# Storing the tokens' 1/rms straight from VectorE's result, number by number

## The chip, the cores and the metric

The kernel runs on one core of a Trainium2 chip. Its engines are TensorE (matmul; PE in the profile), VectorE (DVE), ScalarE (ACT), GpSimd (POOL) and SyncE (SP), each with its own list of instructions that it works off in order, and 16 DMA engines that move data. SP, ScalarE and GpSimd issue DMAs. On-chip data lies in SBUF (128 partitions); TensorE writes into PSUM, which has eight banks of 128 x 512 numbers here. The metric is the device time of one execution in microseconds (us); lower is better.

## What is computed

One layer of a decoder trunk, for 1,024 tokens of 1,024 channels, all in float32. Cut to its core:

```
h = rmsnorm(x, norm_g) * (1 + scale) + shift        # scale, shift, gate from silu(c) @ mod_w
cv, cg, cs, lx, ls = split(h @ w_in)
v = layernorm(depthwise_conv31(cv * sigmoid(cg)))
y_conv = (silu(v) @ pw2 + pw2_b) * silu(cs)
y_lru = scan(gates(depthwise_conv4(lx))) * silu(ls)
x = x + (1 + gate) * (concat(y_conv, y_lru) @ w_out)
return rmsnorm(x, final_g)
```

`rmsnorm` divides each token by the root of its mean square over the channels: x * rsqrt(mean(x * x) + 1e-6). The change is in how those 1,024 numbers, one for each token, get to where they are needed.

## The kernel before

**Layout.** Channels lie on the partitions and tokens along the free dimension: `x` is eight tiles of 128 channels x 1,024 tokens. Each float32 matmul is made of three: weights and activations are split into a high and a low part (`whi`, `wlo`; `uh`, `ul`), and high x high, high x low and low x high are added up in PSUM. One output tile (128 x 1,024, two banks of 512 tokens) takes 2 x 8 x 3 = 48 matmuls of 128 x 512.

**The start.** To keep TensorE busy from the beginning, the first seven tiles of h @ w_in are made without the tokens' 1/rms: `FIRST` (four tiles, `first0` to `first3`, L805) and `NEXT` (`ps4` to `ps6`, L506) multiply x * g * (1 + scale), and 1/rms is multiplied in afterwards, on VectorE, as the product is read out of PSUM (`first_u<-first,rbc`, `next<-ps,rbc`, both L374). The shift's share is a bias, summed in `fsum` on VectorE and added up over channels by TensorE (`psbias`, L1011). From tile 7 on, the activations themselves are normalised: VectorE multiplies x by `rbc` (L366), ScalarE and VectorE split them into `uh` and `ul` again. The second half of `first3` finds no free bank at first; it is computed afterwards as `late`, once ScalarE has copied the first half of `first3` out.

**From the squares to `rbc`.** The steps that the change touches:

- VectorE sums the squares of the eight tiles (`sq`); TensorE sums them over the channels (`token_stats`, L949) into `psb`, 128 tokens x 8 blocks: token b * 128 + p stands on partition p in column b.
- ScalarE takes the root (`st`, L355), VectorE its reciprocal in place (L957).
- TensorE turns `st` round with a matmul by the identity (`turn`, L960): 8 rows of 128 tokens, in the same bank `psb`.
- ScalarE copies the 8 rows out of PSUM into the first rows of `rbc` (L347), and its queue stores them to DRAM (`rrowd`, L964), 8 rows of 512 bytes.
- SP's queue loads the 1,024 numbers back, broadcast to all 128 partitions: `rbc`, 128 x 1,024 (L965, through the helper at L395).

**What sets the order.** The whole program is first written down as operations with an engine, a cost, a priority and what they read and write (`S.op` and the helpers ACT, TT, STT, DMA). The planner (`Plan.order`) then runs them through a list scheduler on its estimated costs and emits every engine's list in the order that comes out. PSUM banks and buffers are given out in that order too, as they come free. A change of a cost or of an operation can therefore move other instructions anywhere behind it. The numbers of the plan around the change: the operation of the store has a cost of 0.3 on ScalarE and a `lag` of 0.1, after which its data counts as written.

The core of it:

```
spread = S.op("PE", 0.2, turn, RSP, [("st", 0)], wk, columns=4 * P)
spread_out = ACT(RSP, row, lambda: psb()[:KT, P:2 * P], "copy", P, r=wk, w=[(rbc, 0)])
S.op("ACT", 0.3, lambda: act.dma_start(flat, row()), RSP, [(rbc, 0)], [("rrowd", 0)], lag=0.1)
DMA(RSP, rbc, lambda: flat.rearrange("b p -> (b p)").partition_broadcast(P), FULL_BYTES,
    r=[("rrowd", 0)], w=[rbc])
```

Of the kernel before, what the change touches and what calls it, by code (L numbers as in the profile page):

```python
# [9 lines left out]
F32 = mybir.dt.float32  # L10
# [4 lines left out]
P = 128  # L15
D = 1024
T = 1024
KT = D // P
# [44 lines left out]
BYPOOL = {512: (0, 1), 768: ()}  # L63
PWE = ((None, None), (None, None), (None, None), ((2, 6), (1, 0)))
REV = -1
OUT_ORDER = (0, 1, 2, 3, 6, 5, 4, 7)
SUMS = (2, 6, 1, 4, 3, 0, 7, 5)
QRES = 0
# [25 lines left out]
SQP, RSP, BIP, HHP, HCH, EVP = -84, -110, -50, -56, 0.1, -80  # L94
# [210 lines left out]
def hymba_layer(ctx: ExitStack, tc: tile.TileContext, xT, xa, vecs, mod_w, mod_s0, w_first, w_pairs, w_in,  # L305
# [3 lines left out]
    act, dve, pool, pe, sp = nc.scalar, nc.vector, nc.gpsimd, nc.tensor, nc.sync  # L309
# [7 lines left out]
    dram = ctx.enter_context(tc.tile_pool(name="dram", bufs=1, space=bass.MemoryType.DRAM))  # L317
# [11 lines left out]
    S = Plan(pools)  # L329
# [11 lines left out]
    def ACT(prio, out, in_, func, n=T, bias=None, scale=None, accum=None, r=(), w=(),  # L341
            reserve=0, after=()):
        kw = {}

        def emit():
            if func == "copy":
                act.copy(out(), in_())  # L347
                return
            if bias is not None:
                kw["bias"] = bias  # L350
            if scale is not None:
                kw["scale"] = scale
            if accum is not None:
                kw["accum_out"] = accum
            act.activation(out=out(), in_=in_(), func=func, **kw)  # L355
        ptr = sum(x is not None and not isinstance(x, float) for x in (bias, scale))
        return S.op("ACT", a_cost(n, ptr) + (0.1 if accum is not None else 0), emit, prio, r, w,
                    table=SETS.get(func), reserve=reserve, after=after)
# [77 lines left out]
    ident = const.tile([P, P], F32, tag="ident", name="ident")  # L436
# [304 lines left out]
    psb = bank("token_stats")  # L741
# [26 lines left out]
    after = []  # L768
    for z, (a, e) in enumerate(CPARTS):
        if e == T:  # L770
            after = [S.op("PE", 0.22 * (e - a) / P, scale_mm, -130,
                          [("cs", 0), *halves(modt[KT], a, e)], [ps_g], after=after, columns=4 * (e - a))]
        after = [S.op("PE", 0.22 * (e - a) / P, lambda z=z: spread_c(z), -130, [("cs", 0)],
                      [ps_c[z]], after=after, columns=4 * (e - a))]
# [43 lines left out]
    for i, ld in enumerate(LOADS):  # L818
        p = due[ld] = i - 100.0
# [5 lines left out]
        elif ld[0] in "wW":  # L825
# [6 lines left out]
                w=keys(rw))  # L832
            for j in range(k, k + nk):
# [3 lines left out]
                for a, e in ((0, FW // 2), (FW // 2, FW)) if j == 0 else ((0, FW),):  # L837
                    ACT(p, fw_part(hi, j, a, e), fw_part(rw, j, a, e), "copy", e - a, r=[(rw, jj)],
                        w=fw_keys(hi, j, a, e))
                if j:  # L840
                    SUB(p, "DVE", fw_part(lo, j), fw_part(rw, j), fw_part(hi, j), FW,
                        r=[(rw, jj), *fw_keys(hi, j)], w=fw_keys(lo, j))
# [35 lines left out]
    for k in range(KT):  # L878
        p = due[f"s{k}"]
# [9 lines left out]
        p = max(p, due[f"x{k}"] if k else p, due[f"w{k}"])  # L889
# [4 lines left out]
        for a, e in START if k < UK else ((0, T),):  # L894
            n = e - a
            hk = halves(x_, a, e)
            if k == 0 == a:
                o = TS(p, part(uh, a, e), part(x_, a, e), g, None, ALU.mult, n=n,
                       r=hk + [("gs", k)], w=halves(uh, a, e))
# [34 lines left out]
    for k in range(KT):  # L934
        p = SQP + k
# [20 lines left out]
               scale=1.0 / D, r=wk, w=[("st", 0)])  # L956
    S.op("DVE", 0.2, lambda: dve.reciprocal(st, st), RSP, [("st", 0)], [("st", 0)])  # L957

    def turn():
        pe.matmul(psb()[:KT, P:2 * P], st, ident, start=True, stop=True)  # L960
    spread = S.op("PE", 0.2, turn, RSP, [("st", 0)], wk, columns=4 * P)
    row, flat = lambda: rbc()[:KT, :P], dram.tile([KT, P], F32, tag="rrow", name="rrowd")
    spread_out = ACT(RSP, row, lambda: psb()[:KT, P:2 * P], "copy", P, r=wk, w=[(rbc, 0)])
    S.op("ACT", 0.3, lambda: act.dma_start(flat, row()), RSP, [(rbc, 0)], [("rrowd", 0)], lag=0.1)  # L964
    DMA(RSP, rbc, lambda: flat.rearrange("b p -> (b p)").partition_broadcast(P), FULL_BYTES,  # L965
        r=[("rrowd", 0)], w=[rbc])

# [359 lines left out]
    for i, (s, ps) in enumerate(zip(FIRST, psf)):  # L1327
        j, p, bi = s[1] % KT, EVP + i, bias[:, i:i + 1]
        t = big_buf(f"first_u{i}", parts=4)
        for a, e in START:  # L1330
            tk, pk, n = halves(t, a, e), halves(ps, a, e), e - a
            if (a, e) in cuts[i]:
                alone = len(cuts[i]) == 1
                if alone:
                    ACT(RSP, part(t, a, e), part(ps, a, e), "copy", n, r=pk, w=tk)
                TT(p - 4 * alone, "DVE", part(t, a, e), part(t if alone else ps, a, e),
                   part(rbc, a, e), ALU.mult, n, r=(tk if alone else pk) + halves(rbc, a, e),
                   w=tk).slack = RBC_LAG
            else:
                late = bank("late")  # L1340
                for k in range(KT):
                    fw_mm(RSP + 60 + 0.1 * k, late, i, uhs[k], uls[k], k, ((a, e),),
                          after=[spread], off=a)
                TT(p, "DVE", part(t, a, e), part(late, 0, n), part(rbc, a, e), ALU.mult, n,
                   r=[late] + halves(rbc, a, e), w=tk)
            if s[1] < CG:
                if a == 0:
                    v[j] = big_buf(f"v{j}")
                STT(p + 3, apart(v[j], a, e), by_two(t, a, e), bi, by_two(sig[j], a, e), ALU.add,
                    ALU.mult, n, r=tk + halves(sig[j], a, e) + [("bias", 0)], w=[v[j]])  # L1350
        if s[1] >= CG:
            ACT(p + 3, t, t, AF.Sigmoid, bias=bi, r=[t, ("bias", 0)], w=[t])
            sig[j] = t
# [303 lines left out]
```

## Time and profile before

| | |
|---|---|
| time, median of 3 runs | 727.56 us (727.23 to 727.83) |
| the profiled execution, its own time | 727.49 us |
| its span, first to last instruction | 725.5 us |
| TensorE's mean granted clock | 0.998 |
| VectorE, ScalarE, GpSimd busy | 87%, 65%, 13% of the span |
| moved by DMA | 112.10 MB |

The profile is one execution. It has the busy time of each engine, the chain of work that ended last (followed back from the last instruction, at each step to what released it), groups of instructions by line, waits, and a timeline. In a timeline's row stand the start, the length, the engine, the line of the kernel, the operation, what it writes and reads (`out<-in`, buffer numbers left out), and in brackets the idle time of the engine ahead of it with what ended it. PEld is the load of weights into TensorE, which overlaps the matmuls. ACTq and SPq are the issues of DMAs. The length of a matmul includes its way through the array, so the pace of a row of matmuls is read from their starts.

### The profile page before, as it was taken

To read this page: it belongs to the slowest core of one execution; us is meant where nothing else is said; L and a number is where in the kernel's file an instruction comes from. 1 tells how busy PE (TensorE), PEld (TensorE's weight loads), DVE (VectorE), ACT (ScalarE), POOL (GpSimd) and SP (SyncE) were. 2 spreads that over 40 slices of the span, in tenths; PEclk is the share of its full clock that TensorE was granted. 3 is DMA by queue.
4 is the path that set the end of the run, shared out by engine and by line. 5 is a ranking of instruction groups with operands and counts; after the bars stand their busy time and mean duration, and the time that the engine had idled before them with its cause. 6 is when DMAs were issued, how large, how long until landed. Compare 5 with 4: busy or idle time off the path is not lost.

```text
span 725.5 us, 8895 instructions
## 1 busy us (share of the span) xinstructions
PE 717.6 (99%) x3250; PEld 597.2 (82%) x3250; DVE 634.4 (87%) x898; ACT 469.9 (65%) x653; POOL 97.5 (13%) x105
## 2 busy tenths in 40 slices
PE   9999999999999999999999999999999999999996
PEld 7888888888888888888888888888888888888886
DVE  6978999999989987787899995998999766997757
ACT  7663766777877878947758885835764334645443
POOL 0042013121232332232021100000000000000001
PEclk9999999999999999999999999999999999999999
DMA  8971026588699799698784545243332530434216
GB/s 334 407 265 63 1 94 136 137 190 190 144 254 239 152 222 221 144 204 169 175 172 101 111 88 161 88 174 134 127 117 77 212 116 2 159 111 137 60 57 232
DMA packets 36634, 112.10 MB, mean 155 GB/s; under 512 B 4072, under 2 KB 10992, under 8 KB 36592
## 3 DMA queue, kind: packets, MB, share of 16 engines
q1 hardware_dynamic: 23760, 76.89, 29.8%
q0 software_dynamic: 12528, 34.26, 26.2%
q8 instruction: 25, 0.41, 0.2%
q10 hardware_dynamic: 304, 0.40, 0.2%
q14 instruction: 17, 0.14, 0.1%
HBM read 64.69 MB, written 12.59 MB: 107 GB/s over the span
## 4 chain that ended last, share of the span: by engine, by line
PE 99%; DVE 0%; ACT 0%; DVEq 0%; issue 0%
PE ps L506 66%; PE first L805 5%; PE pbpw L617 3%; PE pupw L617 3%; PE papw L617 3%; PE gate L1246 3%; PE out L687 2%; PE puout L617 2%; PE paout L617 2%; PE pcpw L617 1%; PE pb0out L617 1%; PE pcout L617 1%; PE late L805 1%; PE out6b L687 1%; PE c_row L757 0%; PE pb1out L617 0%
## 5 line engine op out<-in xcount | busy, mean ns | idle before, releaser
L506 PE MATMUL ps<-uh,whi 128*128 128x512 f32 x576 | 224.2, 389 | 0.0
L506 PE MATMUL ps<-ul,whi 128*128 128x512 f32 x576 | 224.2, 389 | 0.0
L506 PE MATMUL ps<-uh,wlo 128*128 128x512 f32 x576 | 224.2, 389 | 0.0
L506 PEld LDWEIGHTS ps<-uh,wlo 128*128 128x128 f32 x576 | 108.1, 188 | 22.5
L506 PEld LDWEIGHTS ps<-ul,whi 128*128 128x128 f32 x576 | 108.1, 188 | 22.4
L506 PEld LDWEIGHTS ps<-uh,whi 128*128 128x128 f32 x576 | 108.1, 188 | 22.3
L347 ACT CAST whi<-raw 128x1024 fp32r<-128x1024 f32 x46 | 47.9, 1046 | 35.7 <-PE ps L506 30.4
L355 ACT ACT_TABLE_LOAD x47 | 60.3, 1283 | 5.5 <-PE ps L506 3.4
L374 DVE TENSOR_TENSOR wlo<-raw,whi 128x1024 fp32r<-128x1024 f32 x39 | 47.5, 1218 | 17.2 <-ACT whi L347 17.1
L379 POOL DMA_DIRECT2D es<-cq x45 | 39.6, 894 | 152.5 <-ACT cq L355 84.9
L366 DVE SCALAR_TENSOR_TENSOR cacc<-v,V,cacc 128x511 f32<-128x511 f32 (+14 forms) x75 | 55.5, 740 | 0.5
L366 DVE SCALAR_TENSOR_TENSOR caccs<-v,V,caccs 128x511 f32<-128x511 f32 (+6 forms) x70 | 52.1, 744 | 1.4
L366 DVE SCALAR_TENSOR_TENSOR caccs<-c,wsum,caccs 128x511 f32<-128x511 f32 (+6 forms) x70 | 51.9, 741 | 0.6
L379 POOL DMA_DIRECT2D oo<-co x42 | 39.9, 949 | 90.9 <-ACT co L355 61.3
L506 PE MATMUL ps<-yh,wlo 128*128 128x512 f32 x128 | 49.8, 389 | 0.0
L506 PE MATMUL ps<-yh,whi 128*128 128x512 f32 x128 | 49.8, 389 | 0.0
L506 PE MATMUL ps<-yl,whi 128*128 128x512 f32 x128 | 49.8, 389 | 0.0
L374 POOL TENSOR_TENSOR fg<-fg,bc 128x512 f32<-128x512 f32 x2 | 2.5, 1280 | 281.5 <-ACT bc L347 281.5
L366 DVE SCALAR_TENSOR_TENSOR xs<-ps,V,xs 128x512 f32<-128x512 f32 (+3 forms) x48 | 35.7, 743 | 0.2
L355 ACT ACTIVATE cq<-v,V 128x511 f32<-128x511 f32 (+14 forms) x45 | 31.7, 710 | 0.0
L366 DVE SCALAR_TENSOR_TENSOR modw<-modw,sc 128x1024 f32<-128x1024 f32 x23 | 30.1, 1313 | 0.4 <-DMA modw<-in_mod_w_dram 0.4
L355 ACT ACTIVATE cq<-c,wsum 128x512 f32<-128x512 f32 x42 | 29.9, 714 | 0.0
(385 smaller groups left out, 1444.7 us busy)
## 6 DMA issues: line engine op xcount, KB each, us to landing
raw<-in_w_in_dram SPq DMA_DIRECT2D x36, 512.0 KB, 5.2
modw<-in_mod_w_dram SPq DMA_DIRECT2D x23, 512.0 KB, 9.1
raw<-in_w_out_dram SPq DMA_DIRECT2D x10, 512.0 KB, 3.6
scsd<-scs SPq DMA_DIRECT2D x8, 512.0 KB, 3.8
acc<-in_xT_dram SPq DMA_DIRECT2D x8, 512.0 KB, 4.6
accd<-acc SPq DMA_DIRECT2D x8, 512.0 KB, 2.6
rawpw<-in_pw_dram SPq DMA_DIRECT2D x8, 512.0 KB, 3.3
scsr<-scsd SPq DMA_DIRECT2D x8, 512.0 KB, 6.1
```

Of the source, the lines that this page charges most:

```text
L347: act.copy(out(), in_())
L355: act.activation(out=out(), in_=in_(), func=func, **kw)
L366: dve.scalar_tensor_tensor(out=out(), in0=in0(), scalar=scalar, in1=in1(), op0=op0, op1=op1, accum_out=accum)
L374: lambda: e.tensor_tensor(out=out(), in0=a(), in1=b(), op=op), prio, r, w,
L379: return S.op("POOL", ISSUE, lambda: pool.dma_start(out(), a(), accum_op=ALU.add), prio, r, w, lag=RATE * n / T, after=after)
L506: pe.matmul(part(ps, a - off, b - off)(), k3(lhs)()[:, k, :], rhs[k]()[:, a:b], start=(k == 0 and lhs is wh and rhs is xh and (a - off) % ...
L617: pe.matmul(part(ps, 0, c1 - c0)(), half(*lhs)()[:, j * P:j * P + P], half(*rhs)()[:, c0:c1], start=start and j == 0 and z == 0, stop=j == ...
L687: pe.matmul(part(ps, a - off, e - off)(), k3(lhs)()[:, k, :], rhs()[:, i * H + a % H:i * H + a % H + e - a], start=k == KORD[0] and lhs is ...
L805: pe.matmul(part(ps, a - off, b - off)(), fw_part(lhs, k, i * P, i * P + P)(), rhs()[:, a:b], start=k == 0 and lhs is wh and rhs is xh, st ...
L1246: pe.matmul(ps(), lhs()[:, j, :], rhs()[:, c0:c1], start=st == 0, stop=st == 2)
```

## The change

The turn by TensorE and the copy out of PSUM go. The store takes `st` itself, 128 partitions x 8 numbers, and writes each number to its place in the 8 x 128 table in DRAM, so that neighbouring numbers of a partition land 512 bytes apart. The load that broadcasts the table is as before. In the plan the store now has a `lag` of 0.6, and the two operations that were ordered behind the turn or the copy (`late`, and the weights of `NEXT`) are ordered behind the root and the store.

```diff
+SCATTER = 0.6
...
-    def turn():
-        pe.matmul(psb()[:KT, P:2 * P], st, ident, start=True, stop=True)
-    spread = S.op("PE", 0.2, turn, RSP, [("st", 0)], wk, columns=4 * P)
-    row, flat = lambda: rbc()[:KT, :P], dram.tile([KT, P], F32, tag="rrow", name="rrowd")
-    spread_out = ACT(RSP, row, lambda: psb()[:KT, P:2 * P], "copy", P, r=wk, w=[(rbc, 0)])
-    S.op("ACT", 0.3, lambda: act.dma_start(flat, row()), RSP, [(rbc, 0)], [("rrowd", 0)], lag=0.1)
+    flat = dram.tile([KT, P], F32, tag="rrow", name="rrowd")
+    spread_out = S.op("ACT", 0.3, lambda: act.dma_start(flat.rearrange("b p -> p b"), st), RSP,
+                      [("st", 0)], [("rrowd", 0)], lag=SCATTER)
     DMA(RSP, rbc, lambda: flat.rearrange("b p -> (b p)").partition_broadcast(P), FULL_BYTES,
         r=[("rrowd", 0)], w=[rbc])
...
-                          after=[spread], off=a)
+                          after=[root], off=a)
```

The planner moves instructions with it. ScalarE's list from the root on, before (`whi` is the high part of a weight tile, `raw` the tile as loaded, `ghi` the same for the gates; the last number of a name is only a running number, and lines from the store on stand a few further up after the change):

```order
L355 ACTIVATE st_99<-token_stats_120,eps_t_88 128x8
L347 CAST whi4_520<-raw4_442 128x1024
L347 CAST whi7_529<-raw7_476 128x1024
L347 COPY rbc_539<-token_stats_120 8x128
L347 CAST whi8_541<-raw8_482 128x1024
L964 DMA rrowd_100<-rbc_539 8x128
L347 CAST ghi1_551<-graw1_493 128x256
```

and with the change:

```order
L356 ACTIVATE st_99<-token_stats_120,eps_t_88 128x8
L348 CAST whi4_520<-raw4_442 128x1024
L961 DMA rrowd_100<-st_99 128x8x1
L348 CAST whi7_534<-raw7_476 128x1024
L348 CAST whi8_541<-raw8_482 128x1024
L348 CAST ghi1_550<-graw1_493 128x256
```

The store stands behind one cast instead of three, and the copy is gone. VectorE's list where `rbc` is first read, before (`modw3` is the last dot product ahead of it; `next4` the first product of `NEXT`):

```order
L366 SCALAR_TENSOR_TENSOR modw3_406,macc_93<-modw3_406,sc_152 128x1024
L374 TENSOR_TENSOR first_u3_491<-late_543,rbc_539 128x512
L374 TENSOR_TENSOR first_u0_602<-first0_0_171,rbc_539 128x512
L374 TENSOR_TENSOR first_u0_602<-first0_1_202,rbc_539 128x512
L374 TENSOR_TENSOR first_u1_611<-first1_0_173,rbc_539 128x512
```

and with the change:

```order
L367 SCALAR_TENSOR_TENSOR modw3_406,macc_93<-modw3_406,sc_152 128x1024
L375 TENSOR_TENSOR first_u0_596<-first0_0_171,rbc_539 128x512
L375 TENSOR_TENSOR first_u0_596<-first0_1_202,rbc_539 128x512
L375 TENSOR_TENSOR first_u1_602<-first1_0_173,rbc_539 128x512
L375 TENSOR_TENSOR first_u1_602<-first1_1_204,rbc_539 128x512
L375 TENSOR_TENSOR first_u2_613<-first2_0_179,rbc_539 128x512
L375 TENSOR_TENSOR first_u2_613<-first2_1_207,rbc_539 128x512
L375 TENSOR_TENSOR first_u3_491<-late_543,rbc_539 128x512
```

The product of `late` moves from the first place to behind the six others. With it the banks change hands: the bank that `ps4_1` (the second half of tile 4) takes was that of `late`, and is now that of `first0_0`. TensorE's list at the sums of the bias, before:

```order
L506 MATMUL ps6_0_759<-uh1_217,wlo6_613 128x512
L1011 MATMUL psbias_771<-ones_84,fsum_514 128x1 x7
L506 MATMUL ps6_0_759<-uh2_261,whi6_575 128x512
L506 MATMUL ps6_0_759<-ul2_273,whi6_575 128x512
L506 MATMUL ps6_0_759<-uh2_261,wlo6_613 128x512
```

and with the change:

```order
L507 MATMUL ps6_0_756<-uh2_261,wlo6_611 128x512
L507 MATMUL ps6_0_756<-uh3_292,whi6_573 128x512
L507 MATMUL ps6_0_756<-ul3_306,whi6_573 128x512
L507 MATMUL ps6_0_756<-uh3_292,wlo6_611 128x512
L1009 MATMUL psbias_777<-ones_84,fsum_514 128x1 x7
L507 MATMUL ps6_0_756<-uh4_337,whi6_573 128x512
```

The sums stand behind four channel tiles of `ps6_0` instead of two, six matmuls later. Further down, VectorE's and ScalarE's lists differ by neighbours that change places, and TensorE's by three matmuls at two places near its tiles 40 and 41; the load of `rbc` keeps its place on SP.

## The prediction

> **What bounds the kernel now.** I read the page's parts 1 and 4 first (busy time, and the chain that ended last), then what TensorE waited for, then the chain around the changed steps.
>
> ```profile
> span 725.5 us, 8895 instructions
> PE 717.6 (99%) x3250; PEld 597.2 (82%) x3250; DVE 634.4 (87%) x898; ACT 469.9 (65%) x653; POOL 97.5 (13%) x105
> ...
> PE 99%; DVE 0%; ACT 0%; DVEq 0%; issue 0%
> ```
>
> TensorE is busy for 717.6 of 725.5 us, and the chain that ended last is TensorE's own list for 99% of it. A busy engine may still be held up inside its list, so the second view is what it waited for, in the whole span:
>
> ```profile
> PE token_stats L752 <- DVE ones L439: 1.1, 1, 1.1
> PE first L805 <- ACT fhi L347: 0.6, 1, 0.6
> ```
>
> Two waits, both in the first microseconds. So whatever VectorE, ScalarE and the DMA queues do in the middle of this kernel is covered, and a saving there alone is worth nothing. Time is won by taking work out of TensorE's list, and lost by making TensorE wait. The chain around the changed steps, in order of time (start, length, what):
>
> ```profile
> 44.33 2.21 PE first L805 x9
> 46.53 0.32 PE token_stats L960 x2
> 46.85 1.60 PE first L805 x6
> 48.45 5.46 PE late L805 x24
> 53.91 6.12 PE ps L506 x27
> ...
> 77.03 1.46 PE psbias L1011 x14
> 78.49 42.97 PE ps L506 x189
> ```
>
> The turn by TensorE (L960) stands in the chain with 0.32 us. The reader should also see the pace: 42.97 / 189 = 0.227 us per matmul where nothing disturbs, but 1.60 / 6 = 0.267 right behind the turn.
>
> **What the change removes.** Three steps go: the turn, ScalarE's copy out of PSUM, and a row of 8 x 128 numbers as the source of the store. What the turn costs is read from the starts of TensorE's instructions:
>
> ```profile
> 46.13 0.40 PE L805 MATMUL first<-ul,fhi 128*128 128x512 f32 x1
> 46.46 0.39 PE L960 MATMUL token_stats<-ident,st 128*8 128x128 f32 x2
> 46.78 0.51 PE L805 MATMUL first<-uh,fhi 128*128 128x512 f32 x1
> 47.12 0.40 PE L805 MATMUL first<-uh,flo 128*128 128x512 f32 x1
> 47.36 0.40 PE L805 MATMUL first<-ul,fhi 128*128 128x512 f32 x1
> ```
>
> From 46.13 to 47.36 there are three steps of ordinary matmuls, which at 0.227 us would take 0.68; they take 1.23. So the turn and the restart behind it cost 1.23 - 0.68 = **0.55 us** of the chain. Bounds: 0.32 (its own piece), and 0.71 (from 44.33 to 48.45 less fifteen matmuls at 0.227: 4.12 - 3.41, which also counts the restart behind the statistics, and that stays). I take 0.55.
>
> ScalarE's copy (0.26 us, below) is on no chain; ScalarE has idle time in front of it. It is worth nothing to the end.
>
> **What the change moves and adds.** These are the steps from 1/rms to its broadcast, on four engines (ACTq and SPq are the issues of DMAs):
>
> ```profile
> 44.53 1.99 ACT L347 CAST whi<-raw 128x1024 fp32r<-128x1024 f32 x2
> 44.67 0.20 DVE L957 RECIPROCAL st<-st 128x8 f32<-128x8 f32 x1
> 46.88 0.26 ACT L347 COPY rbc<-token_stats 8x128 f32<-8x128 f32 x1 [0.37 <-PE token_stats L960]
> 47.05 1.05 ACT L347 CAST whi<-raw 128x1024 fp32r<-128x1024 f32 x1
> 47.17 0.54 ACTq L964 DMA_DIRECT2D rrowd<-rbc  x1
> 48.47 0.33 SPq L395 DMA_DIRECT2D rbc<-rrowd  x1
> ...
> rbc<-rrowd SPq DMA_DIRECT2D x1, 512.0 KB, 3.5
> ```
>
> Before: result at 44.87, the store is issued at 47.17, the load that spreads it to all partitions waits for the store and goes at 48.47, so the store of 8 rows takes 48.47 - 47.17 = 1.30 us, and rbc lands at 48.47 + 3.5 = 51.97.
>
> After: the store stands behind one cast of `whi4` instead of two casts and the copy. It waits for VectorE's 44.87. The row of 47.17 shows that an issue runs beside a cast already under way (47.05 to 48.10), so I put the issue at 45.0; the bounds are 44.9 and the end of that cast, 45.6. The gain there is 2.2 us. Queued behind the store on ScalarE are the casts of `whi7` and `whi8`, the next at 45.5. If the issue of 1,024 numbers holds ScalarE longer than the 0.54 us of eight rows, the removed copy and its idle time (0.63 us) pay first, and the tile that is waited for, `whi5`, was cast by 51.7 and is read at 53.91 + 48 x 0.227 = 64.8. That is 13 us of reserve, so I cost the issue at nothing.
>
> The store itself is the unknown. Nothing in this trace moves single numbers. It has 1,024 pieces of 4 bytes, 64 for each of 16 DMA engines. The price of a piece comes from two queues:
>
> ```profile
> q1 hardware_dynamic: 23760, 76.89, 29.8%
> q10 hardware_dynamic: 304, 0.40, 0.2%
> ```
>
> q1: 0.298 x 16 x 725.5 us / 23,760 = 146 ns for a packet of 3.2 KB. q10: 0.002 x 16 x 725.5 / 304 = 76 ns for 1.3 KB (57 to 95, since the share has one digit). The line through both meets 0 bytes at about 28 ns (9 to 47). I take 28, since a 4-byte piece is nearest to no bytes: 64 x 0.028 = 1.8 us on top of the 1.30, a store of **3.1 us**. Bounds: 1.3 us (pieces for nothing) and 1.3 + 64 x 0.146 = 10.6 us (each as dear as a packet of 3.2 KB).
>
> rbc then lands at 45.0 + 3.1 + 3.5 = 51.6, against 51.97: the earlier issue pays for the slower store. With the bounds it is 49.8 to 59.1.
>
> **Who waits for rbc.** VectorE alone, and through it TensorE, by the PSUM banks that VectorE frees:
>
> ```profile
> 53.95 0.69 DVE L374 TENSOR_TENSOR first_u<-late,rbc 128x512 f32<-128x512 f32 x1 [4.27 <-PE late L805]
> 54.56 0.68 DVE L374 TENSOR_TENSOR first_u<-first,rbc 128x512 f32<-128x512 f32 x1
> ...
> 64.83 0.69 DVE L374 TENSOR_TENSOR next<-ps,rbc 128x512 f32<-128x512 f32 x1 [1.39 <-PE ps L506]
> 70.27 0.69 DVE L374 TENSOR_TENSOR next<-ps,rbc 128x512 f32<-128x512 f32 x1 [0.34 <-PE ps L506]
> ...
> 88.18 0.69 DVE L374 TENSOR_TENSOR next<-ps,rbc 128x512 f32<-128x512 f32 x1 [0.38 <-PE ps L506]
> 88.79 0.74 DVE L366 SCALAR_TENSOR_TENSOR ul<-x,shift,uh 128x512 fp32r<-128x512 f32 x1
> ```
>
> Before, VectorE sat idle for 4.27 us until 53.95, and not for rbc, which had landed two microseconds earlier, but for `late`. In the new order it begins with `first0_0`, which TensorE has long finished, so VectorE now waits for rbc alone, and starts sooner if rbc lands before 53.95. TensorE needs the bank of `first0_0` for `ps4_1`, 24 matmuls behind `ps4_0`: 53.91 - 0.55 + 24 x 0.227 = 58.8. With 0.68 us for the multiplication and 0.1 for the signal, rbc may land as late as 58.0. My 51.6 leaves 6.4 us. In terms of the store, TensorE waits only if it takes over 58.0 - 45.0 - 3.5 = 9.5 us. What VectorE gains ahead of 64.8 it gives back there, waiting for TensorE: the rows show it idle at 64.83, 70.27 and 88.18 for TensorE's products. So it is worth nothing, and whatever VectorE loses up to 1.39 us is worth nothing either.
>
> On SP, two loads stand behind the broadcast:
>
> ```profile
> 49.64 1.69 SPq L395 DMA_DIRECT2D modw<-in_mod_w_dram  x2
> ...
> modw<-in_mod_w_dram SPq DMA_DIRECT2D x23, 512.0 KB, 9.1
> ...
> 66.17 1.22 DVE L366 SCALAR_TENSOR_TENSOR modw<-modw,sc 128x1024 f32<-128x1024 f32 x1
> ```
>
> They are read from 66.17 on, so with 9.1 us in flight they may be issued as late as 57; the broadcast goes at 48.1 by my sum and at 55.6 by its upper bound.
>
> **The new order elsewhere.** The planner puts the sums `psbias` six matmuls later (6 x 0.227 = 1.36 us, less the 0.55), and VectorE's `v` products behind one more of `next6`. TensorE does the same work. The tightest place is where tile 7 starts. `ul1` is ready at 88.79 + 0.74 = 89.53; TensorE reads it 52 matmuls behind 78.49, at 90.3: 0.8 us of margin. VectorE does the same list between the two waits for TensorE there, and both move earlier by the same 0.55, so I cost it at nothing; without that cover it is at most 1.36 us.
>
> **Sum.** 727.49 us for the profiled execution (span 725.5, 2.0 around it) - 0.55 = 726.94. The median of the three runs, 727.56, is 0.07 above the profiled one, so I predict **727.0 us**, a ratio of 0.9992.
>
> **Rivals.** *The store takes far longer than its pieces' line says.* For it: no row shows a 4-byte piece, and neighbouring pieces of one 512-byte row come from different partitions. Against it: it needs over (9.5 - 1.3) / 64 = 128 ns a piece. It can be worked out as a read and a write for each piece: 2 x 64 x 0.028 + 1.3 = 4.9 us, which hides, but with 0.076 each 11.0 us, which does not. At the bound of 10.6, rbc lands at 59.1, TensorE stands 1.0 us at `ps4_1`, and VectorE runs 5.15 us late, of which TensorE's own shift takes 0.45, the three idle times 2.11 and the margin 0.8: 1.8 us more are lost at tile 7. Then -0.55 + 1.0 + 1.8 = +2.25, 729.8 us; it decides from a store of 9.5 us on.
> The Trainium skill speaks for this rival and against the change: DMA: Bandwidth & Descriptors, section Rules for kernel authors, says that a last dimension that isn't contiguous is lowered to one descriptor per element and should be rearranged, and its Specifications say that below 512 B the DMA engine reads, modifies and writes. By that the store is the 4.9 to 11.0 us above. No run here shows it yet.
>
> *The new order makes TensorE wait.* The sigmoids wait for `psbias`, so VectorE's `v` products could slip by up to 1.36 us, past the margin of 0.8: 0.6 us at tile 7, which cancels the gain: 727.5. For a loss beyond 0.2% it would have to do this at several more places; the whole trace shows no wait in the middle, but its margins there are not all known.
>
> *The turn was free.* If TensorE's restart only moves to the next place, 727.4 to 727.6. Against it: the starts quoted above.
>
> **How the numbers follow.** No change is what a measurement of this kernel can't tell from it, about 0.2% or 1.45 us. The forecast holds 0.60. The cancelled gains, both inside 0.2%, hold 0.12. The slow store holds 0.17 and new waits of 2 us and more 0.05: slower 0.22. A gain of over 1.45 us has no step in the profile that could bring it, since all that leaves the chain is at most 0.71; I leave 0.06 for what the profile doesn't show. So the same has 0.72. The forecast's own range is 726.5 to 727.6 (the bounds of the turn, and 0.3 us of spread); the whole range reaches to the slow store, 726.5 to 729.8.
>
> **What would show it.** Right: the chain's 15 matmuls of `first` in one piece of about 3.5 us; the store issued near 45.0 and the load of rbc near 48; VectorE's first `first_u` before 53.4; no wait of TensorE for VectorE. Wrong: the load of rbc on SP after 54.5, an idle TensorE near 58.8 or 90, or a store's issue that holds ScalarE's casts for microseconds.

## The result, and the profile after

The change made the kernel slower: 731.36 us (median of 7 runs, 730.0 to 734.0) against 727.78 us for the kernel before in the same session (7 runs, 727.23 to 729.09). The ratio is 1.0051, 95% interval 1.0032 to 1.007. The forecast of 727.0 missed by over 4 us and the time lies above the whole range; what happened is the rival of the slow store, and it cost more than that rival allowed.

The profiled execution took 731.36 us with a span of 728.9 (before: 727.49 and 725.5). The page's busy times, its chain and its queue of the small stores:

```profile
PE 719.1 (99%) x3248; PEld 598.5 (82%) x3248; DVE 633.6 (87%) x898; ACT 469.9 (64%) x652; POOL 97.6 (13%) x105
...
q10 hardware_dynamic: 1328, 0.40, 0.2%
...
PE 97%; DMA 2%; DVE 0%; ACT 0%; issue 0%; DVEq 0%; ACTq 0%
```

TensorE is still busy 99% of the span, which says nothing of a loss of 0.5%. The chain does: 2% of it are now DMA. Queue q10 has 1,024 packets more than before, yet its share is unchanged at 0.2%, so the time that the packets took doesn't show what the store cost. The waits of TensorE, in the whole span, have one row that was not there (the other two, in the first microseconds, are those of before):

```profile
PE ps L507 <- DVE first_u L375: 2.5, 1, 2.5
```

The chain around it, in order of time (start, length, what):

```profile
42.93 1.69 PE token_stats L950 x16
...
44.64 9.38 DMA raw<-in_w_in_dram
...
55.02 5.65 DMA rbc<-rrowd
...
60.76 0.70 DVE first_u L375
...
61.51 20.74 PE ps L507 x84
...
83.70 41.61 PE ps L507 x183
125.32 2.72 PE gate L1244 x12
```

Ahead of the load of rbc this chain names raw6's load and its cast, which ended in the same instant; what SP itself waited for is the store. Three rows give the store its length: its issue by ScalarE, the issue of the load that waits for it on SP, and SP's wait (us in total, times, longest):

```profile
45.18 0.40 ACTq L961 DMA_DIRECT2D rrowd<-st  x1
...
55.02 0.33 SPq L396 DMA_DIRECT2D rbc<-rrowd  x1
...
SPq L396 <- DMA rrowd<-st: 9.9, 1, 9.9
```

The store was issued where the forecast had it (45.18 for 45.0), and the load behind it followed 55.02 - 45.18 = **9.84 us** later, for 3.1 forecast. The load of rbc took 5.65 us for 3.5, so VectorE freed the bank of `first0_0` at 60.76 + 0.70, and TensorE, done with `ps4_0`, had stood idle since 58.67 + 0.39. Then comes a second loss, which the waits don't list. TensorE's instructions across the gap:

```profile
58.67 0.39 PE L507 MATMUL ps<-uh,wlo 128*128 128x512 f32 x1
61.51 0.80 PE L507 MATMUL ps<-uh,whi 128*128 128x512 f32 x1 [2.45 <-DVE first_u L375]
...
62.53 0.63 PE L507 MATMUL ps<-uh,wlo 128*128 128x512 f32 x1
62.95 0.63 PE L507 MATMUL ps<-uh,whi 128*128 128x512 f32 x1
...
64.61 0.40 PE L507 MATMUL ps<-ul,whi 128*128 128x512 f32 x1
```

Until 64.6 a matmul starts every 0.43 us instead of every 0.227. The windows say why (length, busy time with instructions of PE, PEld, DVE, ACT and POOL, granted clock, DMA share, GB/s):

```profile
58.60:61.50 2.90, 0.46 (x3) 0.03 (x1) 0.74 (x2) 0.05 (x1) 1.35 (x1) 0.94 0.99 343
61.50:65.00 3.50, 3.49 (x9) 2.82 (x10) 3.50 (x7) 0.00 (x0) 0.00 (x0) 0.57 0.95 390
65.00:70.00 5.00, 5.00 (x24) 4.13 (x23) 4.89 (x11) 1.98 (x6) 0.00 (x0) 1.00 0.01 5
```

Behind the idle stretch the granted clock is 0.57 on average; read in windows of 0.05 us it is 0.50 from 61.1 to 64.5, then 1.00 again. In the chain the 84 matmuls from 61.51 take 20.74 us, where 84 x 0.2274 (41.61 / 183) would be 19.10: 1.64 us. From the first statistics matmul to `gate` TensorE takes 125.32 - 42.93 = 82.39 us, before 121.46 - 42.65 = 78.81, so +3.58: -0.55 for the turn, +2.45 of idle time, +1.64 of slow clock make +3.54. With a start that was 0.28 later, `gate` begins 3.86 us later than before. The two spans differ by less, 3.4 us, since the end behind TensorE's last work was 0.4 us shorter in this execution.

### The profile page after: what moved, and what is told of

Its sections match the earlier page's. It is cut to its first block, busy times and chain, and to the rows that moved or that the text cites. A ratio compares the mean times of both kernels' runs of the same rounds, so it can differ in the third digit from the quotient of the medians.

```text
span 728.9 us, 8895 instructions
## 1 busy us (share of the span) xinstructions
PE 719.1 (99%) x3248; PEld 598.5 (82%) x3248; DVE 633.6 (87%) x898; ACT 469.9 (64%) x652; POOL 97.6 (13%) x105
## 4 chain that ended last, share of the span: by engine, by line
PE 97%; DMA 2%; DVE 0%; ACT 0%; issue 0%; DVEq 0%; ACTq 0%
PE ps L507 65%; PE first L806 5%; PE pbpw L618 3%; PE pupw L618 3%; PE papw L618 3%; PE gate L1244 3%; PE out L688 2%; PE puout L618 2%; PE paout L618 2%; PE pcpw L618 1%; DMA raw<-in_w_in_dram 1%; PE pb0out L618 1%; PE pcout L618 1%; DMA rbc<-rrowd 1%; PE out6b L688 1%; PE c_row L758 0%
## 5 line engine op out<-in xcount | busy, mean ns | idle before, releaser
L367 DVE SCALAR_TENSOR_TENSOR caccs<-v,V,caccs 128x511 f32<-128x511 f32 (+6 forms) x70 | 52.1, 744 | 1.4
L375 POOL TENSOR_TENSOR wlo<-raw,whi 128x1024 fp32r<-128x1024 f32 x7 | 18.2, 2619 | 86.1 <-ACT whi L348 86.1
```

What stands on the lines that cost most here:

```text
L367: dve.scalar_tensor_tensor(out=out(), in0=in0(), scalar=scalar, in1=in1(), op0=op0, op1=op1, accum_out=accum)
L375: lambda: e.tensor_tensor(out=out(), in0=a(), in1=b(), op=op), prio, r, w,
```

## The experiments

All are edits of the kernel after, except the three chains of small DMAs, which are added to the kernel before; those three took 727.17, 727.77 and 728.54 us, one run each. "Stretch" below is the time from the first statistics matmul to `gate` in the chain: 78.81 before, 82.39 in the change.

**Store the numbers as rows, with the statistics strided (`e1_strided`).**

```diff
-            pe.matmul(psb()[:, b:b + 1], sq()[:, b * P:b * P + P], ones[:, 0:1],
+            pe.matmul(psb()[:, b:b + 1], sq()[:, b::KT], ones[:, 0:1],
...
-    flat = dram.tile([KT, P], F32, tag="rrow", name="rrowd")
+    flat = dram.tile([P, KT], F32, tag="rrow", name="rrowd")
...
-    ... act.dma_start(flat.rearrange("b p -> p b"), st)
+    ... act.dma_start(flat, st)
```

> The change with one thing altered: the statistics matmuls take every eighth token, so that a partition's eight numbers are neighbours in DRAM and the store is 128 rows of 32 bytes instead of 1,024 pieces of 4 bytes. The order of the instructions is that of the change on every engine. Theory PIECES (the number of 4-byte writes makes the store 9.8 us): by 1.30 us for 8 rows and the 133 ns/piece per engine that the change showed, 128 rows cost at most 1.3 + 8 x 0.133 = 2.4 us; rbc lands by 52, TensorE waits for nothing after its start, and the time is 726.5 to 727.3. Theory NEIGHBOUR (raw6's load, issued 0.5 us ahead of the store, delays it whatever its pieces are): the store stays near 9.8 us and the time near 731. Theory ORDER (the new order of the instructions costs the time, and the store's wait only stands where it is seen): near 731 with a short store too.

Measured: 731.77 us (5 runs, 730.44 to 732.45), ratio 1.0052 (1.0038 to 1.0066). By its time alone this would be the theory ORDER. The trace tells otherwise: the store took 50.72 - 47.28 = 3.4 us and TensorE waited for nothing behind its start. The time went elsewhere, in the chain (first fence) and in windows (second; columns as above):

```profile
43.14 3.58 PE token_stats L950 x16
46.72 6.10 PE first L806 x15
```

```profile
43.00:47.00 4.00, 4.00 (x18) 4.00 (x18) 1.97 (x6) 1.35 (x5) 0.00 (x0) 0.78 0.08 31
47.00:50.00 3.00, 3.00 (x8) 2.32 (x8) 2.91 (x5) 3.00 (x5) 1.97 (x1) 0.50 0.61 184
```

Loading every eighth column made the 16 statistics matmuls take 3.58 us for 1.69, and during these matmuls of one column, at 45.2, the clock fell to 0.50, where it stayed until 52.1, with TensorE never idle. So this run mends one loss and makes another of about the same size; it decides nothing about the order, and a cleaner one was needed.

**Raw6's load behind the store, not ahead of it (`e3_raw6`).**

```diff
-    DMA(RSP, rbc, lambda: flat ...
+    rbc_load = DMA(RSP, rbc, lambda: flat ...
...
-        weights(s, where="all", late=[...])
+        weights(s, [rbc_load] if s == NEXT[2] else (), where="all", late=[...])
```

> The change with raw6's load issued behind rbc's load instead of 0.5 us ahead of the store; the store keeps its 1,024 pieces. Theory PIECES: store to landing still 8.5 to 10 us, first_u still the only new wait of TensorE, time near 731 or more since raw6 now comes late too. Theory NEIGHBOUR: store about 3 us or less, rbc's load issued by 48.5, no wait for first_u.

Measured: 732.01 us (one run). The wait of SP for the store:

```profile
SPq L396 <- DMA rrowd<-st: 10.1, 1, 10.1
```

The store was issued at 44.84 and the load of rbc at 54.70: 9.86 us, with raw6's load no longer ahead of it. TensorE waited 3.0 us for first_u. This alone does not refute NEIGHBOUR: the planner put a load of modw in raw6's place, of the same 512 KB, issued at 44.08, 0.76 us ahead of the store. The theory falls by two runs below: the store takes 9.24 us with nothing ahead of it (`q1_pieces`), and rows take 3.05 with raw6's load ahead (`e4_rows`).

**What small writes cost by themselves (`q1_pieces`, `q2_spaced`, `q3_lines`).** Each is the kernel before with a chain of stores and reads of DRAM on SP, in a stretch where next to nothing else is transferred (before, 1 GB/s from 72 to 90 us); each waits for the one ahead. Of `q1_pieces`:

```diff
+        sp.dma_start(d0, st)
+        sp.dma_start(r0, d0)
+        sp.dma_start(d1.rearrange("b p -> p b"), r0)
+        sp.dma_start(r1, d1.rearrange("b p -> (b p)").rearrange("(p b) -> p b", b=KT))
+        sp.dma_start(d2.rearrange("b (p z) -> p b z", z=2), r1.rearrange("p (b z) -> p b z", z=2))
+        sp.dma_start(r2, d2.rearrange("b (p z) -> (b p z)", z=2).rearrange("(p b) -> p b", b=KT))
+        sp.dma_start(d3, r2)
+        sp.dma_start(r0, d3)
```

> The kernel before, its own store kept, with a chain of small DMAs added on SyncE's queue in the stretch from about 59 us, where no other DMA runs; each waits for the one ahead, so that the issue times tell how long each took. In turn: 128 rows of 32 bytes stored, read back; 1,024 pieces of 4 bytes, 512 bytes apart on a partition, as in the change, read back; 512 pieces of 8 bytes, read back; 128 rows of 32 bytes again, read back. Theory PIECES: 32-byte rows 1.5 to 2.5 us, the 4-byte store 8.5 to 10 us with nothing beside it, the 8-byte store about half of that (5 to 6 us). Theory NEIGHBOUR: all of the stores near each other, 1.5 to 3 us.

The issues on SP (start, length of the issue); the distance to the next issue is the time of a transfer:

```profile
63.38 0.33 SPq L1408 DMA_DIRECT2D cr<-cd  x1
64.94 0.38 SPq L1409 DMA_DIRECT2D cd<-cr  x1
74.18 0.33 SPq L1410 DMA_DIRECT2D cr<-cd  x1
78.45 0.37 SPq L1411 DMA_DIRECT2D cd<-cr  x1
82.50 0.32 SPq L1412 DMA_DIRECT2D cr<-cd  x1
```

The store of the change, with nothing beside it, takes 74.18 - 64.94 = 9.24 us; 512 pieces of 8 bytes 4.05; 128 rows of 32 bytes, later in the chain, 1.43. Reading the numbers back takes 4.27 us behind the 4-byte store and 1.56 behind the rows. Each of the three chains also begins with 128 rows of 32 bytes, issued 0.38 us behind a load of 512 KB: there they take 3.0 us. So a load just ahead does cost a small store some 1.6 us, far less than the change's store is late.

`q2_spaced` asks whether it is the number of pieces:

```diff
+        sp.dma_start(d1.rearrange("(p b) s -> p b s", b=KT)[:, :, 0:1], r0.rearrange("p (b z) -> p b z", z=1))
...
+        sp.dma_start(d2.rearrange("b p -> p b"), r1[:, :2])
```

> The kernel before with another such chain. In turn: 128 rows of 32 bytes stored, read back; 1,024 pieces of 4 bytes, each alone in a stretch of 64 bytes of DRAM, stored and read back piece by piece; 256 pieces of 4 bytes close together, as in the change but a quarter of them, stored, read back; 128 rows of 8 bytes stored; 1,024 pieces of 4 bytes read from DRAM in the turned order; 128 rows of 32 bytes stored. Theory PIECES: the store of 1,024 spaced pieces takes 8.5 to 10 us as the close ones do, the 256 pieces 3.0 to 3.6 us (1.30 + 16 x 0.133). Theory SHARED LINE (what is slow is that partitions on different DMA engines write into the same few bytes of DRAM): the spaced pieces take 3 us or less. For the reading of 1,024 pieces neither theory has a number; a read that is as slow as the store would say that a piece costs its time whichever way it goes.

```profile
64.63 0.63 SPq L1409 DMA_DIRECT2D cd<-cr  x1
68.65 0.57 SPq L1410 DMA_DIRECT2D cr<-cd  x1
71.07 0.39 SPq L1411 DMA_DIRECT2D cd<-cr  x1
80.60 0.33 SPq L1412 DMA_DIRECT2D cr<-cd  x1
```

It is not. 1,024 pieces of 4 bytes that stand 64 bytes apart take 68.65 - 64.63 = 4.02 us, and 256 pieces that stand close together, a quarter of the change's store, take 80.60 - 71.07 = 9.53, as long as all 1,024. Neither number is what PIECES, as a price for each piece, expected (8.5 to 10, and 3.0 to 3.6). SHARED LINE missed as well: it wanted 3 us or less for the spaced pieces. Reading 1,024 separate numbers of 4 bytes takes 71.07 - 68.65 = 2.42 us, and 2.87 where they lie close together and are read in the change's order, so a read of such pieces is not slow. `q3_lines` then changes the distance alone:

```diff
+    def spaced(s):
+        return df[0:P * KT * s].rearrange("(b p s) -> p b s", b=KT, s=s)[:, :, 0:1]
...
+        for to, src in (... (spaced(2), one), (spaced(4), one), (spaced(8), one), (spaced(32), one), ...):
+            sp.dma_start(to, src)
+            sp.dma_start(cr, df[0:P].rearrange("(p b) -> p b", b=1))
```

> The kernel before with a third chain of small DMAs in the quiet stretch, all stores of 4-byte pieces (but the first and last), a 512-byte read after each. In turn: 128 rows of 32 bytes; 512 pieces 8 bytes apart, a partition's four pieces neighbours; then 1,024 pieces in the change's turned order with 8, 16, 32 and 128 bytes from one to the next; 128 rows of 32 bytes. Known: 4 bytes apart 9.24 us for 1,024 and 9.53 us for 256 pieces; 64 bytes apart (a partition's pieces neighbours) 4.02 us. Theory SHARED LINE, each write into a stretch of 64 bytes waits for the one before: 8 apart about half of 9.2 (4.5 to 5.5 us), 16 apart and above near 4 us. Theory WIDER LINE (512 bytes): 9, 5, 4.5, 4 falls more slowly, 16 and 32 apart still above 4.3 us. Theory ENGINES (it is writes from different partitions that collide): the 512 neighbours' pieces near 2.7 us, under the 4.05 us that 512 pieces of 8 bytes took in turned order.

The stores have L1415, in the order of the expectation; the read behind each has L1416:

```profile
66.06 0.60 SPq L1415 DMA_DIRECT2D cd<-st  x1
70.47 0.33 SPq L1416 DMA_DIRECT2D cr<-cd  x1
72.61 0.37 SPq L1415 DMA_DIRECT2D cd<-st  x1
77.05 0.33 SPq L1416 DMA_DIRECT2D cr<-cd  x1
79.03 0.37 SPq L1415 DMA_DIRECT2D cd<-st  x1
81.91 0.32 SPq L1416 DMA_DIRECT2D cr<-cd  x1
83.87 0.37 SPq L1415 DMA_DIRECT2D cd<-st  x1
86.66 0.32 SPq L1416 DMA_DIRECT2D cr<-cd  x1
88.63 0.37 SPq L1415 DMA_DIRECT2D cd<-st  x1
91.43 0.32 SPq L1416 DMA_DIRECT2D cr<-cd  x1
93.38 0.32 SPq L1415 DMA_DIRECT2D cd<-st  x1
94.78 0.32 SPq L1416 DMA_DIRECT2D cr<-cd  x1
```

| store | pieces | distance in DRAM | us |
|---|---|---|---|
| as in the change (q1) | 1,024 x 4 B | 4 B | 9.24 |
| a quarter of it (q2) | 256 x 4 B | 4 B | 9.53 |
| (q3) | 1,024 x 4 B | 8 B | 4.44 |
| a partition's four are neighbours (q3) | 512 x 4 B | 8 B | 4.41 |
| (q1) | 512 x 8 B | 8 B | 4.05 |
| (q3) | 1,024 x 4 B | 16 B | 2.88 |
| (q3) | 1,024 x 4 B | 32 B | 2.79 |
| (q3) | 1,024 x 4 B | 128 B | 2.80 |
| a partition's eight are neighbours (q2) | 1,024 x 4 B | 64 B | 4.02 |
| rows (q3) | 128 x 32 B | 32 B | 1.40 |

The time follows the distance and not the count: it halves from 4 to 8 bytes, falls to 2.88 at 16 and then stays. That is what one would see if writes waited for one another inside a stretch of DRAM (SHARED LINE), though its numbers were off: it wanted 4.5 to 5.5 us at 8 bytes and near 4 from 16 on. No run shows the waiting itself, nor whether each write is a read and a write there. A stretch of 64 bytes holds 16, 8 and 4 pieces; at 9.24 / 16 = 0.58 us and 4.44 / 8 = 0.56 us for each, four would be 2.3, below the 2.8 that 1,024 scattered pieces cost anyway. The size of the stretch itself isn't settled: any size gives the same ratio. Of WIDER LINE only the figures fall, which were above 4.3 us at 16 and 32 bytes. ENGINES wanted 2.7 us where a partition's own pieces are neighbours; it falls, since they cost as much (4.41) as other partitions' (4.44). One row fits none of these: 64 bytes apart, a partition's pieces neighbours, took 4.02 instead of 2.8.

**The change with rows, nothing else altered (`e4_rows`).** Each number then stands at another token's place.

```diff
-    flat = dram.tile([KT, P], F32, tag="rrow", name="rrowd")
-    ... act.dma_start(flat.rearrange("b p -> p b"), st)
+    flat = dram.tile([P, KT], F32, tag="rrow", name="rrowd")
+    ... act.dma_start(flat, st)
```

> The change with its 1,024 numbers stored as 128 rows of 32 bytes, as VectorE left them, with the statistics as the change has them: the numbers then stand at other tokens than their own, so the output is not the reference's; instructions, their order and their sizes are those of the change. It parts the cost of the store's pieces from that of the new order, which the strided statistics of the run before mixed with a slower stretch of TensorE. Theory PIECES (here and below: 4-byte writes that land among each other's lines are what is late): store 1.4 to 3.5 us (32-byte rows took 1.43 us in the chain of small DMAs, 3.4 us in the strided run), no wait of TensorE after its start, 726.5 to 727.3. Theory ORDER: near 731.

Measured: 726.94 us (11 runs), ratio 0.9989 (0.9977 to 1.0). In the chain TensorE runs through:

```profile
42.56 1.68 PE token_stats L950 x16
...
53.25 24.48 PE ps L507 x108
...
120.79 2.72 PE gate L1244 x12
```

The order is that of the change on every engine, and the time is the forecast's, so ORDER falls. The stretch is 120.79 - 42.56 = 78.23 us, 0.58 less than before: the turn's 0.55. The store took 48.22 - 45.17 = 3.05 us, 0.9 us behind raw6's load; compare the 3.0 us of rows behind a load in the chains.

**The same with the right numbers (`e5_perm`).** The statistics read neighbouring columns again; ScalarE's squares write them in turned order.

```diff
-        ACT(p, sq, xt[k], AF.Square, ...
+        ACT(p, lambda sq=sq: sq().rearrange("d (b p) -> d p b", b=KT),
+            lambda k=k: xt[k]().rearrange("d (p b) -> d p b", b=KT), AF.Square, ...
...
-    flat = dram.tile([KT, P], F32, tag="rrow", name="rrowd")
+    flat = dram.tile([P, KT], F32, tag="rrow", name="rrowd")
...
```

> The same store of 128 rows of 32 bytes, with the right numbers: ScalarE's eight squares write their 1,024 columns in an order turned by eights, so that the statistics matmuls, which read neighbouring columns, put tokens 8p to 8p+7 on partition p. Should the strided writes cost ScalarE nothing: no wait of TensorE, 726.5 to 727.3. Should they slow the squares (1.0 us each) to double, ScalarE's casts come later and TensorE may wait early: 727.3 to 731.

Measured: 727.33 us (11 runs, 726.75 to 728.85), ratio 0.999 (0.9981 to 0.9998). The squares did double:

```profile
L356 ACT ACTIVATE sq<-x x8: 2079/2100/2114, 8.4 to 39.2; 128x1024 f32<-128x1024 f32 x8
```

Before they took 1,048 ns. ScalarE has the time: TensorE waits for nothing in the middle, and the stretch is 78.26 us. This version does what the change meant to, by about 0.1%; against the 0.2% bound of the prediction it is no change, though its interval ends below 1.

**TensorE's wait filled with work (`e6_warm`).**

```diff
+                if s == NEXT[0] and k == nk - 1 and cols == (FULL[0],) and lhs is wh and rhs is xl:
+                    for _ in range(12):
+                        pe.matmul(part(ps, a - off, b - off)(), k3(lhs)()[:, k, :], rhs[k]()[:, a:b],
+                                  start=False, stop=False, skip_group_check=True)
```

> The change with 12 more matmuls, 12 x 0.227 = 2.72 us, at the end of the tile that TensorE finishes at 58.67: they fill the time in which it waits for first_u, and add a product twelve times over, so that the output is not the reference's. Theory CLOCK (after an idle stretch TensorE runs some 3.4 us at about half its clock, which cost 1.64 us): the wait becomes under 0.3 us, the matmuls behind it run at 0.227 us each, the clock in that stretch is 1.00, and the time falls by 1.3 to 1.9 us to 729.5 to 730.1. Rival (the matmuls behind the wait are slow because of what VectorE and the DMA do at that moment, or the lost 3.9 us is otherwise the wait alone): the time stays at 731.0 to 731.7.

Measured: 731.45 us (4 runs), so the rival's number. But in the trace the wait and the slow clock are gone; the chain:

```profile
44.40 1.68 PE token_stats L954 x16
...
60.30 2.72 PE ps L513 x12
63.02 19.27 PE ps L507 x85
...
125.41 2.72 PE gate L1248 x12
```

The stretch is 81.01 us, which is e4's 78.23 and the 2.72 of the added matmuls, with 0.06 left. The 85 matmuls behind run at 0.227 us each. That is 1.38 us better than the change, and the execution had begun 1.47 us later. So both were run again, side by side.

> The change itself, beside the next two on one chip, as the measure for them: 730 to 733, TensorE waiting 2 to 3 us for first_u and then some 3 us at about half its clock.

> The change with TensorE's wait filled by 12 matmuls, again, beside the change: in the first look the wait and the slow stretch were gone and the stretch from the statistics to gate0 was 1.37 us shorter than in the change, but TensorE had begun 1.46 us later, and the time was the change's. Theory CLOCK (the late start belongs to that execution): 1.0 to 1.9 us less than the change. Rival (whatever stands between, the change's time isn't made of the wait and the clock): within 0.5 us of the change, with a start that isn't late.

Measured: the change 732.9 us (6 runs, 730.84 to 735.6; ratio 1.0053 to 1.0087), with the filler 731.13 (5 runs; 1.0035 to 1.0061). The distance of 1.8 us is the one expected, but the intervals overlap, and the two profiled executions lie 1.15 us apart (732.28 and 731.13), so the time alone leaves it unclear. The rows don't: this time the store took longer (first_u came at 61.48 and 61.43), and where the change, idle for 3.6 us, then falls to half its clock, the filled one is idle for 1.02 and stays at 1.00:

```profile
61.50:65.00 3.50, 2.78 (x9) 2.21 (x10) 3.50 (x6) 0.00 (x0) 0.00 (x0) 0.75 1.02 407
65.00:70.00 5.00, 5.00 (x20) 4.04 (x19) 4.90 (x10) 1.86 (x6) 0.00 (x0) 0.83 0.13 54
```

```profile
61.50:65.00 3.50, 2.83 (x12) 2.36 (x13) 3.50 (x6) 0.00 (x0) 0.00 (x0) 1.00 1.00 411
```

The first fence is the change, the second the filled kernel. The 0.75 and 0.83 are means: in windows of 0.05 us the change's clock is 1.00 until 63.3, 0.50 until 66.7, and 1.00 behind that. VectorE and the DMA are as busy in both (3.50 us, 407 and 411 GB/s), so it isn't they that slow the matmuls down. In the filled kernel TensorE also waits once for `ul` at tile 7, for 0.16 us.

**The right length in the plan (`e2_lag9`).**

```diff
-SCATTER = 0.6
+SCATTER = 9.0
```

> The change with the planner told that the store takes 9.0 us instead of 0.6: modw6's load is issued ahead of rbc's load, and VectorE is given other work first; the pieces stay. Theory PIECES with a late load: the store is still issued near 45 and landed near 55, since its pieces are the same; rbc's load has one modw load behind it instead of two and lands 3.5 to 5.7 us later, at 58.4 to 60.5; TensorE waits 0.4 to 2.5 us for first_u, and the time is 728 to 731: a right figure in the plan gets back a part at most. Rival (the plan's wrong figure, not the pieces, is what cost the time): no wait of TensorE, 726.9 to 727.5.

Measured: 732.92 us (6 runs, 730.3 to 737.47), ratio 1.0075 (1.0052 to 1.0097). The store took 11.32 us (45.02 to 56.34), the load 5.6, and TensorE waited 3.9. So telling the planner 9.0 did not make it put other work ahead of the bank; whether another order could cover the store was not tried. The time falls outside the expected range too, on the upper side: the store was the longest of these runs, and modw6's load, issued at 45.67, now runs beside it, which may be why.

**The loads behind rbc's held back (`e7_hold`).**

```diff
+    def rbc_load():
+        sp.dma_start(rbc(), flat.rearrange("b p -> (b p)").partition_broadcast(P))
+        sp.dma_start(seen, rbc()[0:1, :KT])
...
```

> The change with a small store of eight numbers of rbc on SyncE's queue right behind rbc's load: it waits for that load to land, and so the loads of modw and raw behind it no longer run beside rbc's load. Theory SHARE (rbc's load takes 5.65 us instead of 3.5 because those loads share the DMA engines with it): the store of the pieces stays at 9.8 to 11.3 us, rbc's load falls to 2 to 3.5 us, TensorE's wait for first_u falls by about 2 us, to 0 to 1.5, and the time by 2 us or more, to 728 to 730.5, since the slow stretch of the clock should go with the wait. Rival (the load is long because it reads lines that were just written in pieces): it stays near 5.6 us, and the time at 731 to 733; a read of 32-byte rows right behind the close pieces had taken 4.27 us in the first chain, where a read behind 32-byte rows took 1.56 us.

Measured: 732.08 us (5 runs), ratio 1.0047 (1.003 to 1.0063). The load of rbc, now with nothing behind it, took 4.52 us (chain: issue 56.35); the store 10.74, so that TensorE still waited 2.2 us and the time did not fall as expected: it is the rival's. Of the 2.15 us that the load had grown by, about half goes with the loads behind it, and neither theory has the whole. The 1.0 us that stays fits the slow read-back of 4.27 us in `q1_pieces`, and `e1_strided` fits it too: there SP issued nothing for 3.48 us behind the load of rbc, which read rows, and it took 3.6 us instead of 4.52. These are single executions with other transfers beside them, so the parting is rough.

## Why the prediction was wrong

*The bound and the turn: right.* TensorE's list is what sets the end, and -0.55 for the turn and its restart is what the stretch shows when nothing else is disturbed: -0.58 in `e4_rows`, -0.55 in `e5_perm`.

*The issue and ScalarE's casts: right.* 45.18 for 45.0, and the 1,024-piece issue held ScalarE's queue for 0.40 us, not longer than the 0.54 of eight rows.

*The price of a piece: the step that failed.* The prediction took 28 ns, "since a 4-byte piece is nearest to no bytes", from packets that each fill bytes of their own. Its bounds of 9 to 47 ns were worked out wrong: with 57 and 95 ns for the second point the line meets 0 bytes at -4 and 61 ns. But 61 would make the store 5.2 us, still under 9.5, so that slip is not what failed. For pieces that lie apart the price was nearly right: in the change's order 1,024 of them 16 to 128 bytes apart take 2.79 to 2.88 us, for 3.1 forecast, with nothing beside them. In the kernel the 1.30 us that the sum starts from was short too: rows issued 0.9 us behind raw6's load took 3.05 (`e4_rows`), and that this equals the forecast is luck. The earlier issue so gained next to nothing even there: the load of rbc went at 48.22, before at 48.47. But the change's pieces stand 4 bytes apart, and those behave as if each waited for the one before: 9.24 us alone, 9.3 to 11.3 in the kernel. No price per piece can give that, since 256 cost what 1,024 do. The prediction had even written down that neighbouring pieces of one row come from different partitions, and gave it no mechanism. The Trainium skill's rule, quoted there (DMA: Bandwidth & Descriptors, section Rules for kernel authors: one descriptor per element where the last dimension isn't contiguous), warned of this very store. The 9.84 us lie inside the 4.9 to 11.0 that the prediction worked out with a read and a write for each piece, but a price for each descriptor is not what the runs show: the 1,024 scattered pieces are as many and take 2.8.

*The load of rbc: mis-sized.* 3.5 us taken over from before, 5.65 measured, 4.52 with the loads behind it held back. With 5.65 the store could have taken 7.35 us, not 9.5, before TensorE waits.

*The place of the stall: right; its price: wrong.* TensorE waits at `ps4_1`, at 59.06 for the 58.8 worked out, and for first_u. The rival's 1.0 us there became 2.45. The 1.8 us that it saw at tile 7 did not come: the waits show none. In its stead stand 1.64 us of slow clock, a term that the prediction does not have. Sum by the measured terms: -0.55 + 2.45 + 1.64 = +3.54, against +3.58 in the trace.

*The new order: right to cost nothing* (`e4_rows`: same order, 726.94).

## What to carry to other kernels

Before a store is turned "for free" by its address pattern, look at which bytes lie beside each other in DRAM: 4-byte pieces that fill a row one by one from many partitions took 9 us for 1 to 4 KB, where the same number of pieces 16 bytes apart or more takes 2.8 us, and rows of 32 bytes 1.4. Make the numbers neighbours on the partition instead, upstream, on an engine with time to spare: here ScalarE's squares, doubled and hidden. And when TensorE is the bound, price a wait of 2.2 us or more at more than itself: here 2.45 us idle cost 4.1. Where between 1.02 and 2.2 us the second loss begins, no run shows.

## What the runs showed of the hardware

- **The clock after an idle stretch.** 1.02 us idle (`e6_warm_again`) left the granted clock at 1.00. Behind idle stretches of 2.2 (`e7_hold`), 2.45 (the change), 3.0 (`e3_raw6`), 3.6 (`c1_change_again`) and 3.9 us (`e2_lag9`) it was 0.50 for one stretch of 3.4 us, no longer behind the longer ones. It fell between 0.4 us ahead of the restart (the change) and 1.4 us behind it (`e2_lag9`), so a window's mean can hide it. The 84 matmuls behind the gap lost 1.64 to 1.90 us by it. The Trainium skill (TensorE: Matmul & The Clock Gate, Part 1) says that the clock is halved after an idle window of about 3.4 us and restored after a busy one. The halved pace, 0.43 us for 512 columns, agrees, and so do the 3.4 us until it is restored; idle stretches of 2.2 and 2.45 us were enough here.
- **The clock without an idle stretch.** In `e1_strided` sixteen matmuls of one column with strided weights, 3.58 us in which TensorE counts as busy, came with a clock of 0.50 for 6.8 us, from 2.1 us behind their start. The same sixteen in 1.68 us did not.
- **Strides in the on-chip memory.** Weights of every eighth column took 335 ns to load for 192, and ScalarE's squares with outputs 512 bytes apart 2,100 ns for 1,048.
- **A neighbour's completion comes late.** In the change raw6's load, issued at 44.64, was seen to land at 54.02 (the chain's 9.38 us), though nothing was moved any more from 50 on:

```profile
50.00:53.00 3.00, 3.00 (x14) 2.46 (x14) 0.00 (x0) 1.29 (x4) 3.00 (x2) 1.00 0.00 0
```

Its cast of whi6 waited 2.81 us for that and finished in time. In `e4_rows`, with the same order and rows in the store, the same cast ran at 50.83 without a wait. So here the slow store of small pieces went with a late landing of a load that has nothing to do with it; how the chip orders the two was not tried.
